# The last layer's loop over further expert tiles, moved from behind the last tile to in front of it

## The chip, the cores and the metric

The kernel runs on one core of a Trainium2 chip. The metric is device time in microseconds (us) of one execution. Three timed runs of the kernel before gave a median of 1104.19 us (1102.88 to 1104.58). The kernel is written in Python on a framework that orders the instructions of each engine with a scheduler of its own and sets all semaphores.

## The reference

The reference is a diffusion backbone of two layers over 256 latent tokens and 256 context tokens of width 1024, in float32. Each layer modulates and normalises its input, projects it, runs three groups of attention heads in parallel, projects back and adds with a layer norm. Then comes the part that this change is about, a mixture of experts with a second residual and layer norm:

```python
g_idx = argmax(h @ w_rg + b_rg)                   # one of 4 groups per token
top_v, top_i = top_k(expert logits in the group, 2)   # two of its 8 experts
combine = one_hot(expert_id, 32) * (softmax(top_v) * g_w), summed over the two
for e in range(32):
    hidden = silu(h @ w1[e]) * (h @ w3[e])        # 1024 -> 256
    out = out + combine[..., e:e+1] * (hidden @ w2[e])  # 256 -> 1024
x = layer_norm(ALPHA * x + g2 * out) * ln2_g + ln2_b
```

In the last layer only the 256 latent tokens go through it, and x is the output.

## The kernel before

**Tiles.** The mixture is computed on the tokens that chose each expert and no others. `passes(l)` lists the tiles of a layer (`todo`): each has 128 rows, shared by one, two or four experts with 128, 64 or 32 slots each. The last layer has 12 tiles, 0 to 11; tile 9 holds four experts, tiles 10 and 11 two each. Tiles go in pairs (`sets`); a pair shares a gathered input `xg` and one-hot rows `ohs`, of which there are two each, used in turn, so that pair 4 (tiles 8 and 9) has number 0 and pair 5 (tiles 10 and 11) number 1.

**One tile.** `up` (L1196) multiplies the gathered tokens with w1 and w3 of the tile's experts into a PSUM bank (L1202) and applies SiLU (L1208, L1209). `mid` (L1232) transposes the result (L1236, L1237). `back` (L1212) makes the matrix that returns rows to tokens (L1220, L1222) and the rows' weights (L1225, L1228). `down` (L1254) multiplies with w2 (L1260), weights the result (L1264) and splits it into two parts (L1265, L1266). `combine` (L1274) adds it to the residual stream X through products (L1282) and VectorE (L1289, or L1286 with sums for the layer norm, at the end). In the last layer the combine of tile i - 1 is written behind `up` of tile i, and that of tile 11 at the end. Then come the layer norm (L414 to L431) and the store (L1580).

**Weights.** An expert has three chunks of 1 MB: two of w1 and w3 (c = 0, 1), one of w2 (c = 2). They are loaded by indirect DMA on the POOL queue (L142), in the order of the tiles, into units of on-chip memory (class `Mem`, 23 units of 1 MB). `pump` issues the next ones while units are free and the cap is kept; `rel` gives a chunk's units back as soon as the tile is through with it and pumps. All loads of tiles 10 and 11 are written ahead of tile 10. At tile 10 `rows` loads two rows for the layer norm (L1463), on the POOL queue too in the last layer; some buffers of the other pair are freed just before.

**Further tiles.** If an expert has more tokens than its slots, the rest goes through a loop whose number of passes is known only on the chip: `rest` (L1494) loads it into a register on each engine (L1498) and runs a device loop (L1499). One pass finds an expert and its tokens, loads three chunks one after the other into one buffer `dyn`, and does up, mid, back, down and combine for 128 rows. The buffer is the unit of the last tile's first w2 chunk, which isn't given back at the tile's end (L1524) but behind the loop. With these inputs the loop makes no pass in the profiled execution; what is left of it are its register loads, branches and the waits at its exit, all recorded at L1498 and L1499.

**Order.** The scheduler orders instructions within the straight parts of the program; the loop divides the program into what is issued before it and what after. Within these it may issue a later instruction first where an earlier one isn't ready.

Of the kernel before, what the change touches and what calls it, by code (L numbers as in the profile page):

```python
# [117 lines left out]
def backbone(ctx: ExitStack, tc, ins, out):  # L118
# [8 lines left out]
    def bank(tag):  # L127
        return ps.tile([128, 512], F32, name="ps" + tag, tag=tag, bufs={"a": 4, "c": 2, "e": 2}[tag])

    def scratch():  # L130
        return sm.tile([128, 512], F32, name="scr", bufs=5)


    stream, slot = [], {}
# [6 lines left out]
    def dyn_load(b, idx):  # L141
        G.indirect_dma_start(out=b.ap(UNIT), out_offset=None, in_=wexp_rows,  # L142
                             in_offset=bass.IndirectOffsetOnAxis(ap=idx, axis=0),
                             bounds_check=NL * NE * 384 - 1, oob_is_err=False)

    def pump(limit=None):
        if limit is not None:
            cap[0] = limit
        while ahead[0] < len(stream):
            key, ap, n = stream[ahead[0]]  # L150
            if ap is None and key[1] not in idx_of:
                return
            if sum(x.g for x in slot.values()) + n // ROW > cap[0] * (UNIT // ROW):
                return
            b = mem.alloc(n)
            if b is None:
                return
            if ap is None:
                dyn_load(b, idx_of[key[1]][:, key[2], key[3]:key[3] + 1])
            else:  # L160
                SP.dma_start(out=b.ap(n), in_=ap)
            slot[key] = b
            ahead[0] += 1

    def take(key):
        if key not in slot:
            pump()
        return slot[key]

    def drop(key):  # L170
        slot.pop(key).free()
# [287 lines left out]
    def layer(l, first, before=None, after=None, rest_of=None):  # L459
        nb = 4 if l == 0 else 2  # L460
        nq = 128 * nb
        last = l == NL - 1
# [616 lines left out]
        for b in range(nb + lag):  # L1079
# [4 lines left out]
            if b >= lag:  # L1084
                c = b - lag
# [22 lines left out]
        xg = [mem.get(8 * 256) for _ in range(2)]  # L1108
        yo = [] if last else [mem.get(D) for _ in range(3)]
        split_y = {}  # L1110

        def parts(i):

            i = 0 if last and i < 2 else i
            if i not in split_y:
                split_y[i] = mem.get(2 * D, F32R)
            yy = split_y[i]
            return yy.v(2, 512), yy.v(2, 512, off=D)
# [3 lines left out]
        ohs = [mem.get(nb * 256, F32R) for _ in range(2)]  # L1122
# [43 lines left out]
        def onehot(q, tiles):  # L1166

            OH = ohs[q % len(ohs)].v(nb, 128 * len(tiles))
            parts = [(m, col, i * 128, 128) for i, (m, col) in enumerate(tiles)]
            if len(parts) == 2 and parts[0][0] == parts[1][0] and parts[1][1] == parts[0][1] + 128 // parts[0][0]:  # L1170
                parts = [parts[0][0:3] + (256,)]
            for b in range(nb):
                for m, col, o, n in parts:
                    e = n // m
                    V.tensor_tensor(OH[:, b, o:o + n].rearrange("p (e s) -> p e s", s=m),  # L1175
                                    iota128[:, None, 0:m].to_broadcast([128, e, m]),
                                    rk[:, b, col:col + e, None].to_broadcast([128, e, m]), OP.is_equal)

        def gather(q, n, jj):

            n *= 128
            OH, XG = ohs[q % len(ohs)].v(nb, n), xg[q % len(xg)].v(8, n)
            p = bank("c")
            pv = p[:, 0:2 * n].rearrange("p (j s) -> p j s", j=2)
            for j in range(2):
                k = jj + j
                for b in range(nb):
                    for i, H in enumerate((HHI, HLO)):
                        PE.matmul(pv[:, j, :], lhsT=H[b][:, k * 128:(k + 1) * 128], rhs=OH[:, b, :],  # L1189
                                  start=(b == 0 and i == 0), stop=(b == nb - 1 and i == 1))  # L1190
            S.activation(XG[:, jj:jj + 2, :], pv, AF.Copy)  # L1191

        def slots(m):
            return [slice(i, i + m) for i in range(0, 128, m)]

        def up(q, at, n, m, W, rel):  # L1196

            XG = xg[q % len(xg)].v(8, 128 * n)
            g = bank("a")
            for k in range(8):  # L1200
                for t, r in enumerate(slots(m)):
                    PE.matmul(g[r, :], lhsT=XG[:, k, at * 128 + r.start:at * 128 + r.stop],  # L1202
                              rhs=W(t, k // 4).v(4, 512)[:, k % 4, :], start=(k == 0), stop=(k == 7))
                if k % 4 == 3:
                    rel(k // 4)
            hab = scratch()
            ha, hb = hab[:, 0:256], hab[:, 256:512]
            S.activation(ha, g[:, 0:256], AF.Silu)  # L1208
            V.tensor_tensor(hb, ha, g[:, 256:512], OP.mult)  # L1209
            return hb  # L1210
# [244 lines left out]
        qe = len(sets) - 1  # L1455
# [17 lines left out]
        def fetch():  # L1473

            for b in range(nb):
                acc[b] = mem.get(D)
                ACC[b] = acc[b].v(D)
                two.append(mem.get(D))
                for dst, j in ((ACC[b], 0), (two[b].v(D), 1)):
                    G.indirect_dma_start(out=dst, out_offset=None, in_=ys[:, :],  # L1480
                                         in_offset=bass.IndirectOffsetOnAxis(ap=find[:, b, j:j + 1], axis=0),
                                         bounds_check=at_row, oob_is_err=False)
# [11 lines left out]
        def rest(dyn, par):  # L1494

            oht.append(mem.get(nb * 128, F32R))
            parts(2)
            r = nc.values_load(lpi[0:1, 0:1], min_val=0, max_val=32)  # L1498
            with tc.For_i(0, r, 1):  # L1499
                further(35)  # L1500

                def load(c):
                    if c < 3:
                        dyn_load(dyn, idx[:, NE, c:c + 1])

                load(0)
                onehot(par, [(128, 35)])
                for jj in range(0, 8, 2):
                    gather(par, 1, jj)
                hb = up(par, 0, 1, 128, lambda t, c: dyn, lambda c: load(c + 1))  # L1510
                ws = back(par, 0, 1, 128, 35, 2)
                down(mid(hb), ws, 128, lambda t, c: dyn, lambda c: None, 2)
                combine([2])

        end = len(todo) - 1
        for i, (m, col, e, _, go) in enumerate(todo):
            q, at_ = i // 2, i % 2
            n = len(sets[q])

            def W(t, c):  # L1520
                return take(("exp", l, e + t, c))

            def rel(c):
                if go and (i != end or c < 2):  # L1524
                    for t in range(128 // m):
                        drop(("exp", l, e + t, c))
                    pump()

            if i == end - 3:
                cap[0] = HC[0] if not last else cap[0] - 2  # L1530
            if i == end - 1:
                for k in [xg.pop((qe + 1) % 2), ohs.pop((qe + 1) % 2)] + yo:
                    k.free()
                if last:
                    rows()
                else:
                    cap[0] = HC[1]
                    rows_g2()
            if i == end:
                cap[0] = HC[2] if not last else 12  # L1540
            if at_ == 0 and q < qe:
                onehot(q + 1, [x[0:2] for x in sets[q + 1]])
            if i == away and away:
                fetch()
            hb = up(q, at_, n, m, W, rel)
            if i and not away:
                combine([(i - 1) % 2])
            if i == away and away:
                fold()
                rows()  # L1550
            if i == 1:
                lists()
            pieces = [jj for jj in range(4 * at_, 4 * at_ + 4, 2) if q < qe]
            if i < away and pieces:
                gather(q + 1, len(sets[q + 1]), pieces.pop(0))
            hc = mid(hb)
            for jj in pieces:
                gather(q + 1, len(sets[q + 1]), jj)
            if i < away:
                put(i, hc, m, W, rel)  # L1560
            else:
                ws = back(q, at_, n, m, col, i % 2)
                down(hc, ws, m, W, rel, i % 2)
        held = [("exp", l, e + t, 2) for t in range(128 // m)]
        rest(slot[held[0]], qe % 2)
        for k in held:
            drop(k)
        pump()
        fin = [end % 2] if last else [0, 1]
        combine(fin, range(2), True)  # L1570
        for k in [iw] + xg + ohs + hh + [oht.pop(2), split_y.pop(2)]:
# [121 lines left out]
```

## Time and profile before

| | |
|---|---|
| median of three runs | 1104.19 us (1102.88 to 1104.58) |
| the profiled execution, whole | 1108.46 us |
| its span in the profile | 1106.6 us, 14809 instructions |
| mean granted TensorE clock | 0.961 |
| busy: TensorE / VectorE / ScalarE / POOL | 998.9 / 512.7 / 349.3 / 305.2 us |
| moved by DMA | 300.54 MB, mean 272 GB/s |

All times in the rows are microseconds from the start of the span, unless marked ns. PE is TensorE's product, PEld its load of weights into the array, DVE VectorE, ACT ScalarE, POOL GpSimd, SP the sync engine; a q behind the name is the engine's sequencer, which waits, branches and issues DMAs. What stands behind an arrow `<-` ended an engine's idle time. The clock column PEclk is the share of full speed that TensorE was granted.

### The profile page before, as it was taken

The page shows a single profiled execution, that of the slowest core. Times are in us where ns is not written, and L with a number is a line of the kernel's source. Part 1 is how long each engine was busy: PE and PEld are TensorE (multiplying, and loading weights), DVE is VectorE, ACT ScalarE, POOL GpSimd, SP SyncE. Part 2 cuts the span into 40 slices and gives each one's busy share as a digit, 9 for nine tenths or more (in the row PEclk, how much of TensorE's full clock was granted, in tenths as well). Part 3 has the DMA queues.
Part 4 walks back from the last instruction along what each step waited for, and adds up shares of the span by engine and source line. Part 5 has one row for each costly group of instructions (what it writes and reads, how often), then busy time and mean ns, then how long its engine had stood idle before and what let it go on. Part 6 is the DMA issues. An engine that isn't in the chain of part 4 may idle for free. (4 is left out here: it accounts for less than half of the span.)

```text
span 1106.6 us, 14809 instructions
## 1 busy us (share of the span) xinstructions
PE 998.9 (90%) x5525; PEld 577.0 (52%) x5525; DVE 512.7 (46%) x1364; ACT 349.3 (32%) x708; POOL 305.2 (28%) x325
## 2 busy tenths in 40 slices
PE   4899999999999999999983789999997899999894
PEld 2689744466866454444430378844466554433231
DVE  4653457775567211100016687267655654242244
ACT  3543155572442011111111385144544222111111
POOL 2021143340000433243333132042300045334420
PEclk9999999999999999999996889999987899999997
DMA  9813147601169999999999653446325799999992
GB/s 372 321 37 115 48 181 275 230 27 51 76 267 374 398 400 423 351 412 422 423 422 414 235 183 119 172 162 216 127 78 232 302 378 421 421 422 420 422 420 94
DMA packets 46208, 300.54 MB, mean 272 GB/s; under 512 B 5395, under 2 KB 5779, under 8 KB 14389
## 3 DMA queue, kind: packets, MB, share of 16 engines
q0 software_dynamic: 25824, 177.81, 39.2%
q1 hardware_dynamic: 20308, 121.75, 29.3%
q8 instruction: 45, 0.74, 0.3%
q14 instruction: 31, 0.25, 0.1%
HBM read 292.19 MB, written 7.34 MB: 271 GB/s over the span
## 5 line engine op out<-in xcount | busy, mean ns | idle before, releaser
L142 POOL DMA_INDIRECT u<-in_w_exp,u x162 | 162.5, 1003 | 305.5 <-PE psa L1202 100.1
L1202 PE MATMUL psa<-u,u 128*32 128x512 f32 (+2 forms) x1040 | 218.1, 602 | 23.8 <-DMA u<-in_w_exp,u 23.7
L1202 PEld LDWEIGHTS psa<-u,u 128*32 128x32 f32 (+2 forms) x1040 | 65.5, 127 | 152.7 <-issue 110.6
L455 PE MATMUL psa<-u,u 128*128 128x512 f32 (+3 forms) x400 | 142.8, 360 | 0.9 <-ACT u L504 0.7
L456 PE MATMUL psa<-u,u 128*128 128x512 f32 (+3 forms) x400 | 141.7, 355 | 2.0 <-DVE u L450 2.0
L457 PE MATMUL psa<-u,u 128*128 128x512 f32 (+3 forms) x400 | 140.3, 354 | 0.1
L1189 PEld LDWEIGHTS psc<-u,u 128*128 128x128 f32 x640 | 83.6, 198 | 33.2 <-issue 30.1
L1189 PE MATMUL psc<-u,u 128*128 128x256 f32 x640 | 94.3, 298 | 3.0 <-DVE u L1175 2.1
L887 POOL TENSOR_SCALAR u<-u,ri 128x512 f32<-128x512 f32 (+1 forms) x48 | 68.5, 1431 | 99.2 <-DVE ri L885 81.7
L1209 DVE TENSOR_TENSOR scr<-scr,psa 128x256 f32<-128x256 f32 x26 | 10.9, 421 | 168.5 <-ACT scr L1208 168.5
L456 PEld LDWEIGHTS psa<-u,u 128*128 128x128 f32 x400 | 77.3, 193 | 12.9 <-DVE u L450 4.2
L455 PEld LDWEIGHTS psa<-u,u 128*128 128x128 f32 x400 | 77.1, 193 | 11.5 <-ACT u L504 1.1
L457 PEld LDWEIGHTS psa<-u,u 128*128 128x128 f32 x400 | 76.5, 192 | 9.8 <-issue 1.2
L884 ACT ACTIVATE u<-psa,nm 128x512 f32<-128x512 f32 (+1 forms) x96 | 58.4, 615 | 55.0 <-DVE nm L882 50.1
L1260 PE MATMUL pse<-u,scr 128*64 128x512 f32 (+1 forms) x288 | 67.4, 599 | 0.6 <-DMA u<-in_w_exp,u 0.6
L1208 ACT ACTIVATE scr<-psa 128x256 f32<-128x256 f32 x26 | 10.0, 385 | 175.8 <-PE psa L1202 175.8
L450 DVE TENSOR_TENSOR u<-u,u 128x1024 fp32r<-128x1024 f32 (+4 forms) x38 | 56.2, 1485 | 19.5 <-ACT u L449 19.4
L1191 ACT ACTIVATE u<-psc 128x512 f32<-128x512 f32 x52 | 31.1, 597 | 101.9 <-PE psc L1189 59.6
L882 DVE TENSOR_REDUCE nm<-psa 128x1 f32<-128x512 f32 (+1 forms) x80 | 53.2, 683 | 13.1 <-PE psa L872 9.5
L1247 PE MATMUL pse<-u,scr 128*32 128x512 f32 (+2 forms) x232 | 57.3, 600 | 1.4 <-ACT scr L1237 1.4
L419 POOL TENSOR_TENSOR lns<-lns,mhalf 128x1 f32<-128x1 f32 x22 | 15.3, 699 | 156.4 <-DVE lns L418 126.2
L449 ACT ACTIVATE u<-u 128x1024 fp32r<-128x1024 f32 (+4 forms) x38 | 47.5, 1266 | 14.2 <-PE psa L456 4.6
(317 smaller groups left out, 1361.6 us busy)
## 6 DMA issues: line engine op xcount, KB each, us to landing
u<-in_w_mod SPq DMA_DIRECT2D x48, 1024.0 KB, 6.0
u<-in_w_exp SPq DMA_DIRECT2D x30, 1024.0 KB, 7.2
u<-in_w_out SPq DMA_DIRECT2D x8, 1024.0 KB, 4.8
ys<-u SPq DMA_DIRECT2D x12, 512.0 KB, 8.1
u<-in_w_in_b SPq DMA_DIRECT2D x10, 512.0 KB, 11.8
u<-in_w_in_v SPq DMA_DIRECT2D x4, 960.0 KB, 4.6
u<-in_w_in_qa SPq DMA_DIRECT2D x4, 768.0 KB, 11.4
u<-in_ln_rows SPq DMA_DIRECT2D x6, 512.0 KB, 7.1
```

What stands on the lines that cost most here:

```text
L142: G.indirect_dma_start(out=b.ap(UNIT), out_offset=None, in_=wexp_rows, in_offset=bass.IndirectOffsetOnAxis(ap=idx, axis=0), bounds_check=N ...
L450: V.tensor_tensor(l_[:, c], w[:, c], h[:, c].bitcast(F32), OP.subtract)
L455: PE.matmul(p, lhsT=a[0], rhs=b[0], start=first, stop=False)
L456: PE.matmul(p, lhsT=a[0], rhs=b[1], start=False, stop=False)
L457: PE.matmul(p, lhsT=a[1], rhs=b[0], start=False, stop=final)
L882: V.tensor_reduce(out=nm[:, s, 0:n], in_=pv, axis=AX.X, op=OP.max, negate=True)
L884: S.activation(P[:, i, :], pv[:, i, :], AF.Exp, bias=nm[:, s, i:i + 1], accum_out=su[:, s, i:i + 1])
L887: (G if s == 0 else V).tensor_scalar(P[:, i, :], P[:, i, :], ri[:, s, i:i + 1], None, op0=OP.mult)
L1189: PE.matmul(pv[:, j, :], lhsT=H[b][:, k * 128:(k + 1) * 128], rhs=OH[:, b, :], start=(b == 0 and i == 0), stop=(b == nb - 1 and i == 1))
L1202: PE.matmul(g[r, :], lhsT=XG[:, k, at * 128 + r.start:at * 128 + r.stop], rhs=W(t, k // 4).v(4, 512)[:, k % 4, :], start=(k == 0), stop=(k ...
L1247: PE.matmul(y[r, :], lhsT=hc[:, c * 128 + r.start:c * 128 + r.stop], rhs=W(t, 2).v(2, D)[:, c, f * 512:f * 512 + 512], start=(c == 0), sto ...
L1260: PE.matmul(y[r, :], lhsT=hc[:, c * 128 + r.start:c * 128 + r.stop], rhs=W(t, 2).v(2, D)[:, c, f * 512:f * 512 + 512], start=(c == 0), sto ...
```

## The change

In the last layer the loop over further tiles is written at the start of the pass for tile 11, ahead of its `up`, and no longer behind its `down`. It uses the unit of tile 10's first w2 chunk, so tile 10 keeps its w2 chunks (`keep`) until the loop is behind it, and tile 11 gives all of its own back. The loop gathers into the buffers of pair 4 instead of those of pair 5, so these aren't freed at tile 10 in the last layer. The first layer keeps its loop behind the last tile.

```diff
--- before.py
+++ after.py
@@ -1512,7 +1512,15 @@
                 down(mid(hb), ws, 128, lambda t, c: dyn, lambda c: None, 2)
                 combine([2])
 
+        def further_tiles(held, par):
+            rest(slot[held[0]], par)
+            for k in held:
+                drop(k)
+            pump()
+
         end = len(todo) - 1
+
+        keep = end - 1 if last else end
         for i, (m, col, e, _, go) in enumerate(todo):
             q, at_ = i // 2, i % 2
             n = len(sets[q])
@@ -1521,7 +1529,7 @@
                 return take(("exp", l, e + t, c))
 
             def rel(c):
-                if go and (i != end or c < 2):
+                if go and (i != keep or c < 2):
                     for t in range(128 // m):
                         drop(("exp", l, e + t, c))
                     pump()
@@ -1529,7 +1537,7 @@
             if i == end - 3:
                 cap[0] = HC[0] if not last else cap[0] - 2
             if i == end - 1:
-                for k in [xg.pop((qe + 1) % 2), ohs.pop((qe + 1) % 2)] + yo:
+                for k in yo if last else [xg.pop((qe + 1) % 2), ohs.pop((qe + 1) % 2)] + yo:
                     k.free()
                 if last:
                     rows()
@@ -1542,6 +1550,8 @@
                 onehot(q + 1, [x[0:2] for x in sets[q + 1]])
             if i == away and away:
                 fetch()
+            if i == end and last:
+                further_tiles(held, (qe + 1) % 2)
             hb = up(q, at_, n, m, W, rel)
             if i and not away:
                 combine([(i - 1) % 2])
@@ -1556,16 +1566,15 @@
             hc = mid(hb)
             for jj in pieces:
                 gather(q + 1, len(sets[q + 1]), jj)
+            if i == keep:
+                held = [("exp", l, e + t, 2) for t in range(128 // m)]
             if i < away:
                 put(i, hc, m, W, rel)
             else:
                 ws = back(q, at_, n, m, col, i % 2)
                 down(hc, ws, m, W, rel, i % 2)
-        held = [("exp", l, e + t, 2) for t in range(128 // m)]
-        rest(slot[held[0]], qe % 2)
-        for k in held:
-            drop(k)
-        pump()
+        if not last:
+            further_tiles(held, qe % 2)
         fin = [end % 2] if last else [0, 1]
         combine(fin, range(2), True)
         for k in [iw] + xg + ohs + hh + [oht.pop(2), split_y.pop(2)]:
```

## Rows read from the trace of the kernel before

**Rows 1.** The page: busy time of each engine, and DMA share in 40 slices.

```profile
PE 998.9 (90%) x5525; PEld 577.0 (52%) x5525; DVE 512.7 (46%) x1364; ACT 349.3 (32%) x708; POOL 305.2 (28%) x325
...
DMA  9813147601169999999999653446325799999992
```

**Rows 2.** Busy time by stretch, with count, clock and DMA share, tile 11.

```profile
core 0: us, PE busy (x) PEld busy (x) DVE busy (x) ACT busy (x) POOL busy (x), PEclk, DMA share, GB/s
1072.20:1083.00 10.80, 10.39 (x40) 3.55 (x38) 4.51 (x7) 1.27 (x3) 0.00 (x0) 1.00 0.96 395
```

**Rows 3.** Timeline of PE, tiles 10 and 11: start, us, line, what.

```profile
1068.47 3.70 PE L1260 MATMUL pse<-u,scr 128*64 128x512 f32 x16
...
1073.62 2.29 PE L1282 MATMUL psa<-u,u 128*128 128x512 f32 x7 [0.21 <-DVE u L1266]
1075.84 7.08 PE L1202 MATMUL psa<-u,u 128*64 128x512 f32 x30
1083.85 0.44 PE L1236 MATMUL psa<-ident,scr 128*128 128x128 f32 x2 [0.93 <-DVE scr L1209]
...
1084.82 3.70 PE L1260 MATMUL pse<-u,scr 128*64 128x512 f32 x16
1090.62 1.19 PE L1282 MATMUL psa<-u,u 128*128 128x512 f32 x4 [2.10 <-ACTq L1499]
```

**Rows 4.** Timeline of DVE at the end.

```profile
1074.34 2.56 DVE L1289 TENSOR_TENSOR u<-u,psa 128x512 f32<-128x512 f32 x4
...
1091.62 0.69 DVE L1266 TENSOR_TENSOR u<-scr,u 128x512 fp32r<-128x512 f32 x1 [1.70 <-PE psa L1282]
1092.22 0.68 DVE L1286 SCALAR_TENSOR_TENSOR u<-psa,u 128x512 f32<-128x512 f32 x1
...
1094.47 0.69 DVE L1286 SCALAR_TENSOR_TENSOR u<-psa,u 128x512 f32<-128x512 f32 x1
```

**Rows 5.** Waits of SP at the end: us in total, times, longest.

```profile
SPq L1499 <- DMA u<-in_w_exp,u: 184.2, 2, 181.7
...
SPq L1499 <- DVEq L1498: 5.0, 1, 5.0
...
SPq L1499 <- DMA u<-in_ln_rows: 2.3, 2, 1.2
```

**Rows 6.** The loop's line, 1040 to 1095: durations in ns, first and last start.

```profile
L1499 PEldq EVENT_SEMAPHORE  x13: 51/51/51, 1088.6 to 1090.3; - x13
```

**Rows 7.** Timeline of POOL at the end.

```profile
1062.90 0.99 POOL L142 DMA_INDIRECT u<-in_w_exp,u  x1 [1.49 <-DMA u<-in_w_exp,u]
...
1067.37 0.55 POOL L1463 DMA_DIRECT2D u<-in_ln_rows  x1 [1.64 <-DMA u<-in_w_exp,u]
```

**Rows 8.** DMA issues from 1000 on: KB each, median us to landing.

```profile
u<-in_ln_rows POOLq DMA_DIRECT2D x2, 512.0 KB, 17.1
...
u<-in_w_exp,u POOLq DMA_INDIRECT x26, 19.1
```

**Rows 9.** Timeline of PE in the first layer, by that layer's loop.

```profile
605.63 6.13 PE L1202 MATMUL psa<-u,u 128*64 128x512 f32 x14 [1.80 <-DMA u<-in_w_exp,u]
```

**Rows 10.** Busy time by stretch there (columns as in rows 2).

```profile
586.00:602.00 16.00, 0.13 (x2) 0.13 (x2) 12.03 (x11) 3.44 (x3) 5.86 (x5) 0.63 1.02 415
606.00:610.60 4.60, 4.60 (x12) 1.18 (x9) 0.00 (x0) 0.00 (x0) 0.00 (x0) 0.50 0.72 297
610.60:612.00 1.40, 1.16 (x4) 0.14 (x1) 0.00 (x0) 0.20 (x1) 0.00 (x0) 0.98 0.00 0
```

**Rows 11.** The loop's line in the first layer.

```profile
L1499 POOLq EVENT_SEMAPHORE  x13: 43/43/11182, 597.6 to 619.7; - x13
```

**Rows 12.** DMA issues from 895 to 900.

```profile
u<-in_w_exp,u POOLq DMA_INDIRECT x2, 9.0
```

**Rows 13.** The page: DMA issues of the whole span.

```profile
u<-in_w_out SPq DMA_DIRECT2D x8, 1024.0 KB, 4.8
```

## The prediction

> **What bounds the kernel now.** I read the page first. TensorE is busy nine tenths of the span, and the DMA engines are full in most slices from the middle of the kernel on, down to the last but two [rows 1]. The change is in the last layer's mixture of experts alone, so I then read its last 50 us by stretches and line by line. While tile 11 (the last one) goes through its up product, TensorE is busy 10.39 of 10.80 us and the DMA engines 0.96 of the time [rows 2]: both are near full, and the DMA stream of expert weights runs out only then. Tile 11 is three steps on TensorE: up (L1202, from 1075.84 for 7.08 us), the small products from L1236 on (1083.85), down (L1260, 1084.82 for 3.70 us, to 1088.52) [rows 3]. Behind it stands the loop over further tiles, which makes no pass here: TensorE next does the combine products (L1282) at 1090.62, after 2.10 us of idleness that the profile puts to L1499, the loop's line. VectorE closes the chain: four final adds (L1286) from 1092.22, the last one at 1094.47 [rows 4], then the layer norm and the store.
>
> The view that decides is the one of waits on SP. SP has nothing to do between its arrival at the loop and the end of the kernel, so it shows what the loop's exit waits for: 184.2 us on two landings of expert weights (longest 181.7), 2.3 us on the two landings of the norm rows (L1463), and 5.0 us on VectorE's reaching the loop [rows 5]. So a loop that makes no pass still holds its engines until every DMA that was issued in front of it has landed, loads that the loop doesn't use included. TensorE runs the same 13 waits [rows 6]. In the kernel before these landings cost nothing: the norm rows are the last DMA, issued at 1067.37 with 17.1 us to landing, so at about 1084.5, while TensorE arrives at 1088.52 [rows 3, 7, 8].
>
> **The change part by part.** The loop moves from behind tile 11 to in front of its up product.
>
> *Removed at the end.* Without the loop the end of tile 11 runs like the end of tile 10. There the down products end at 1072.17 (1068.47 + 3.70) and the first L1289 add starts at 1074.34, 2.17 us later; behind the loop the same step (1088.52 to 1092.22) takes 3.70 us [rows 3, 4]. The four L1286 take 2.95 us with a gap (to 1095.17); without one, as the four L1289 show (2.56 us, plus a last accumulator read of about 0.1), 2.65. So the end gains (3.70 - 2.17) + (2.95 - 2.65) = 1.83 us. Between 1.5 (the gap stays) and 2.1 (all of TensorE's idleness).
>
> *Added in front of tile 11.* TensorE is through with tile 10 at 1072.17. POOL has by then issued every load of tile 11 and both norm rows (the last load at 1062.90, the last row at 1067.37, [rows 7]); these stand ahead of the loop in the source of both, and their buffers don't depend on tile 11. So the loop's exit waits for all of them, to 1084.5. The rows' landings are not the last of the 13 waits; the engines' own stand behind them, some seven, at 0.051 us each plus issue and a branch, which I take as 0.9 us in all (between 0.4, seven waits by their own durations, and 2.1, the whole idleness of before; the first is nearer, since the engines have long arrived) [rows 3, 6]. TensorE starts again at about 1085.4. It has idled for 13.2 us.
>
> *Its clock.* The other loop place shows the like: in layer 0 TensorE did 0.13 us of work from 586 to 602, waiting for weights, and the 14 up products from 605.63 ran in 6.13 us at a granted clock of 0.50 (the 1.2 GHz level) up to 610.6, then at 0.98 [rows 9, 10]. So about 5 us of work at half rate, which loses 2.4 us. Between 0 (the clock stays) and 3.8 (the whole up product at half rate for 7.5 us).
>
> *Tile 11 behind the loop.* Up takes 7.5 us (32 products; the timeline shows 30 in 7.08 [rows 3]), 9.9 with the clock, so it ends at 1095.3. The combine products of tile 10 (8 of L1282, 2.5 us; seven took 2.29) ran in front of tile 11's up; they write the stream that the loop's combine also writes, so they come behind the loop now. They can fill the 0.93 us that TensorE idles before L1236 and push the rest back by 1.6 us (between 0, if the adds and copies around hide them, and 2.5). From up's end to the end of down is 5.60 us (1082.92 to 1088.52), all weights being there. Down ends at 1095.3 + 1.6 + 5.6 = 1102.5 in place of 1088.5: 14.0 us later. No cover is left to lose here: VectorE and ScalarE wait for TensorE throughout.
>
> *The buffers.* The weights' buffer lent to the loop is tile 10's and not tile 11's; two units stay held a little longer, and two gather buffers and one-hot sets aren't freed before the norm rows are allocated. All weights have been issued by then, so nothing is delayed by it; I take 0 (at worst the row that lands last comes one load step of 2.48 us later, which would add that much to the loop's wait; at best it lands that much earlier). Layer 0 keeps its loop where it is: 0.
>
> *Sum.* + 14.0 - 1.8 = + 12.2 us on the profiled execution, whose span is 1106.6 us and whose whole time, 1108.46, is 4.3 us above the median 1104.19 of the runs shown. On the median: 1104.2 + 12.2 = 1116.4. With the low ends (clock 0, combine hidden) it is + 8.2, so 1112.4; with the high ends of clock, combine and exit + 15.7, so 1119.9.
>
> **The rivals.** What is written in front of the loop needn't be issued in front of it: L1266 at 1091.62 runs behind the loop and is written before it [rows 4], because the program's order is a scheduler's.
>
> *The last loads slip behind the loop.* Then the landings in front of it are over when TensorE arrives, its exit costs 2.1 us as before (1074.3), and POOL issues the last four loads (those up to 1062.90) only then. Two loads into a queue that had just run empty took 9.0 us to land [rows 12] and further ones follow at the step of 2.48 us: the second half of up can start at 1074.7 + 9.0 + 2.5 = 1086.2, takes 3.6 us (to 5.4 at the low clock), 1.9 more to down, and 3.7 for down: 1095.4 to 1097.2, so + 5.0 to + 6.8 after the gain at the end, 1109.2 to 1111.0. For it: the L1266 above. Against: POOL had those loads out 9 us before TensorE got there, and L1266 lagged because its input wasn't ready, while these buffers are free.
>
> *They slip, and land fast.* The page's direct loads of the same 1 MB took 4.8 us to land [rows 13]; at that price the same case comes out 4.2 us lower, 1105.0 to 1106.8. Against it stands the 9.0 of the very kind of load [rows 12]. The Trainium skill (DMA: Bandwidth & Descriptors, Anatomy of one DMA) puts one DMA of POOL's path at 2.0 us plus its bytes over 436 GB/s, an estimate of 4.4 us for 1 MB, by which this case would be some 0.4 us lower still.
>
> *The loop slides back.* The scheduler runs tile 11 in front of it, so that it doesn't do what it says. Only tile 10's combine then comes later, four L1289 (2.56 us) on the chain: 1106.8. Against: the up product's bank would have to pass the loop's own.
>
> *The exit doesn't hold for DMAs* (the other side). If TensorE leaves after engines alone, at 1074.3, the loads stream on under it; up then starts 0.5 to 1.4 us late (part of the combine falls into later idleness) and the end gains 1.8: - 0.4 to - 1.3, so 1102.9 to 1103.8, and 1102.1 at best if the exit's 2.1 us are all saved. It decides from the point where the waits of SP on landings turn out to be SP's alone. For it: nothing waited for these DMAs before but SP and POOL. Against: TensorE has the same 13 waits, and in layer 0 POOL stood 11.18 us in one wait of that line [rows 11].
>
> **How the numbers follow.** The forecast gets 0.70, the slipped loads 0.09, those that land fast 0.03, the loop that slides back 0.10, the exit without landings 0.08. The time is the likeliest's, 1116.4. A range of 1108.5 to 1120.0 takes in the forecast's own (1112.4 to 1119.9) and the slipped loads, and leaves the other three out, which is 0.21. A measurement of this kernel tells about 0.2% (2.2 us) from no change: slower is the forecast, the slipped loads and half of the sliding loop, 0.84; faster 0.03, out of the exit without landings; the rest, 0.13, within.
>
> **What would show it.** In the changed kernel TensorE should idle from the end of tile 10's down products for some 13 us, with L1499 or the rows' landing as its releaser; the up products behind it should run at a granted clock of 0.5 at first; L1282 should follow the last down products within about 1 us, and no L1499 should stand there. POOL should show its last weight load at about 1063 as before. The prediction is wrong if TensorE passes the loop before 1083, or if weight loads are issued after it.

## The result, and the profile after

The changed kernel takes 1113.66 us (median of four runs, 1112.04 to 1114.05), the kernel before 1104.21 beside it (four runs, 1102.88 to 1104.58). The ratio is 1.0085, with a 95% interval of 1.0068 to 1.0102: 9.45 us slower (7.5 to 11.3). The forecast was 1116.4, in a range of 1108.5 to 1120.0, with 0.84 on slower.

The profiled execution of the changed kernel took 1112.04 us whole, with a span of 1110.3. That of before lay 4.3 us above its own median, so the two can't be subtracted as they stand: in front of the change both run the same instructions in the same order, and the run of before is 7.1 us late there. It is also later than every other execution in this document (they reach that point between 1061.35 and 1065.24); no run looked for the reason. All comparisons below therefore start from one point, the first down product of tile 10 (L1260 at 1068.47 before [rows 3], at 1061.35 after), and count from there to the end of the span: 38.11 us before, 48.91 after, which is + 10.80. Line numbers are the same in both kernels up to the loop; behind it they shift (the store is L1589).

The page of the changed kernel first, with the lines that answer to [rows 1] (busy time of each engine, DMA share in 40 slices):

```profile
PE 994.4 (90%) x5525; PEld 574.8 (52%) x5525; DVE 512.4 (46%) x1364; ACT 349.0 (31%) x708; POOL 304.4 (27%) x325
...
DMA  9722157510369999999998643365327799999970
```

The busy times are those of before within half a per cent: no work was added. The last DMA slice fell from 2 to 0: the stream ends at the same place, and what follows it has become longer.

Next, the timeline of TensorE (start, us, engine, line, what, and in brackets the idle time before it with its releaser), which answers to [rows 3]:

```profile
1061.35 3.70 PE L1260 MATMUL pse<-u,scr 128*64 128x512 f32 x16
1078.41 8.95 PE L1202 MATMUL psa<-u,u 128*64 128x512 f32 x32 [13.36 <-issue]
1087.29 2.12 PE L1282 MATMUL psa<-u,u 128*128 128x512 f32 x8
1089.26 0.38 PE L1236 MATMUL psa<-ident,scr 128*128 128x128 f32 x2
...
1090.42 3.65 PE L1260 MATMUL pse<-u,scr 128*64 128x512 f32 x16
1094.01 1.10 PE L1282 MATMUL psa<-u,u 128*128 128x512 f32 x2
1095.93 1.64 PE L1282 MATMUL psa<-u,u 128*128 128x512 f32 x6 [0.82 <-ACT u L1265]
```

TensorE idles 13.36 us between tile 10's down and tile 11's up. The profile names no releaser for it ("issue"), though it named L1499 for the idle time at the loop before [rows 3]. The chain of waits says who it was; it is followed back from the first up product (start, us, what):

```profile
1059.90 0.34 DVE scr L1209
1060.23 17.11 DMA u<-in_ln_rows
1077.35 1.06 issue
1078.41 8.95 PE psa L1202 x32
```

The second norm row, issued at 1060.23, lands at 1077.35, and TensorE starts 1.06 us later. That TensorE itself stands in these landings shows at the loop's line, the view that answers to [rows 6] (durations in ns: least, median, most; then first and last start):

```profile
L1499 PEldq EVENT_SEMAPHORE  x13: 51/51/1027, 1065.1 to 1078.1; - x13
```

One of its 13 waits now takes 1.03 us, where before none took more than 0.051; by the trace it ends with the second row's landing, and seven more waits stand behind it. SP's waits agree, the view that answers to [rows 5] (engine, line, what it waited for: us in all, times, longest):

```profile
SPq L1499 <- DMA u<-in_w_exp,u: 183.3, 2, 180.9
...
SPq L1499 <- DMA u<-in_ln_rows: 2.3, 2, 1.2
```

The waits on landings are those of before; the 5.0 us on VectorE's reaching the loop has gone, since VectorE now gets there before the DMAs are through. POOL's timeline, which answers to [rows 7]:

```profile
1055.76 0.98 POOL L142 DMA_INDIRECT u<-in_w_exp,u  x1 [1.51 <-DMA u<-in_w_exp,u]
1058.01 0.57 POOL L1463 DMA_DIRECT2D u<-in_ln_rows  x1 [1.26 <-DMA u<-in_w_exp,u]
1060.23 0.55 POOL L1463 DMA_DIRECT2D u<-in_ln_rows  x1 [1.65 <-DMA u<-in_w_exp,u]
```

The last weight load is issued 5.58 us ahead of tile 10's down products, as before (1062.90 against 1068.47). Nothing slipped behind the loop.

The clock behind the pause is in the table of stretches (columns as in [rows 2]):

```profile
1065.05:1078.40 13.35, 0.00 (x0) 0.00 (x0) 2.04 (x3) 1.25 (x2) 0.00 (x0) 0.63 0.82 336
1078.40:1080.00 1.60, 1.59 (x4) 0.53 (x6) 0.00 (x0) 0.00 (x0) 0.00 (x0) 0.50 0.01 5
...
1081.00:1082.00 1.00, 1.00 (x6) 0.35 (x4) 0.00 (x0) 0.00 (x0) 0.00 (x0) 0.50 0.00 0
1082.00:1087.40 5.40, 5.40 (x27) 1.63 (x23) 0.00 (x0) 0.00 (x0) 0.00 (x0) 0.98 0.00 0
```

TensorE starts again at a granted clock of 0.50 (the 1.2 GHz level) and has it for some 3.6 us; then it is at the 2.4 GHz level. At the end VectorE's timeline, which answers to [rows 4]:

```profile
1088.17 2.47 DVE L1289 TENSOR_TENSOR u<-u,psa 128x512 f32<-128x512 f32 x4
...
1095.14 0.69 DVE L1286 SCALAR_TENSOR_TENSOR u<-psa,u 128x512 f32<-128x512 f32 x1
...
1096.93 0.69 DVE L1286 SCALAR_TENSOR_TENSOR u<-psa,u 128x512 f32<-128x512 f32 x1 [0.33 <-PE psa L1282]
...
1098.16 0.69 DVE L1286 SCALAR_TENSOR_TENSOR u<-psa,u 128x512 f32<-128x512 f32 x1
```

From the end of down (1094.07) to the end of the last L1286 (1098.85) it takes 4.78 us, where before it took 6.65 (1088.52 to 1095.17): the loop's crossing at the end has gone. The parts have changed too: the first add comes 1.07 us behind down (before 3.70), and the four adds take 3.71 us (before 2.95), with 1.10 us between the first and the second.

### The profile page after: what moved, and what is told of

Its sections match the earlier page's. It is cut to its first block, busy times and chain, and to the rows that moved or that the text cites. A ratio compares the mean times of both kernels' runs of the same rounds, so it can differ in the third digit from the quotient of the medians.

```text
span 1110.3 us, 14804 instructions
## 1 busy us (share of the span) xinstructions
PE 994.4 (90%) x5525; PEld 574.8 (52%) x5525; DVE 512.4 (46%) x1364; ACT 349.0 (31%) x708; POOL 304.4 (27%) x325
## 5 line engine op out<-in xcount | busy, mean ns | idle before, releaser
L1202 PE MATMUL psa<-u,u 128*32 128x512 f32 (+2 forms) x1040 | 217.1, 605 | 35.1 <-DMA u<-in_w_exp,u 21.7
L1202 PEld LDWEIGHTS psa<-u,u 128*32 128x32 f32 (+2 forms) x1040 | 66.0, 128 | 163.4 <-issue 125.3
L1209 DVE TENSOR_TENSOR scr<-scr,psa 128x256 f32<-128x256 f32 x26 | 10.9, 421 | 179.4 <-ACT scr L1208 179.4
L1260 PE MATMUL pse<-u,scr 128*64 128x512 f32 (+1 forms) x288 | 67.3, 599 | 0.6 <-DMA u<-in_w_exp,u 0.6
```

The source lines that it names most:

```text
L1260: PE.matmul(y[r, :], lhsT=hc[:, c * 128 + r.start:c * 128 + r.stop], rhs=W(t, 2).v(2, D)[:, c, f * 512:f * 512 + 512], start=(c == 0), sto ...
```

## The experiments

Two theories were put against each other. **Landings:** the exit of a loop that makes no pass holds every engine until all DMAs issued in front of it have landed, so the price is set by the last landing. **Fixed price:** leaving the loop there costs a stall of its own (registers, branches, a restart), whatever the queue holds. The first five columns count from the first L1260 of tile 10, in us of one profiled execution each, and the ratio is against the kernel before on the same chip. For the change that is the pair above. The median of before, of 23 runs each, is 1101.74 us beside four of the kernels (the rows behind the loop, one more load, before without its loop, the loop in front of down) and 1103.0 beside the other four. The ratio isn't the quotient of the two medians; it differs from that by up to 0.001.

| kernel | up starts | up takes | down starts | last add ends | span ends | timed: median, ratio (95%) |
|---|---|---|---|---|---|---|
| before | 3.48 | in two parts | 16.34 | 26.69 | 38.11 | 1104.21 |
| the change | 17.07 | 8.95 | 29.08 | 37.50 | 48.91 | 1113.66, 1.0085 (1.0068 to 1.0102) |
| rows behind the loop | 15.08 | 8.55 | 26.68 | 35.10 | 46.54 | 1109.81, 1.0071 (1.0051 to 1.0091) |
| one more load in front | 19.64 | 8.86 | 31.56 | 39.98 | 51.48 | 1115.35, 1.0114 (1.0094 to 1.0133) |
| before, no loop | 3.48 | in two parts | 16.34 | 24.87 | 36.59 | 1101.68, 0.999 (0.9978 to 1.0002) |
| the change, no loop | 3.48 | in two parts | 16.34 | 24.86 | 36.57 | 1101.77, 0.9985 (0.9971 to 0.9999) |
| loop in front of down | 3.49 | in two parts | 18.39 | 26.82 | 38.24 | 1103.51, 1.0006 (0.999 to 1.0021) |
| products in front of the loop | 17.03 | 7.09 | 27.18 | 35.60 | 47.01 | 1111.96, 1.0085 (1.0069 to 1.0101) |
| weights behind the loop | 5.83 | in four parts | 26.14 | 34.66 | 46.08 | 1111.29, 1.0073 (1.0052 to 1.0094) |
| loop in front of mid | 3.49 | in two parts | 17.39 | 27.58 | 39.02 | 1103.06, 0.9995 (0.9981 to 1.0009) |

**The norm rows behind the loop.** This takes the last two landings away from the loop: the loads that land last in the changed kernel are issued behind it, and land while up runs.

```diff
                 if last:
-                    rows()
+                    pass
...
                 further_tiles(held, (qe + 1) % 2)
+                rows()
             hb = up(q, at_, n, m, W, rel)
```

> The changed kernel, with the two norm rows' loads written behind the loop. Theory (landings): the loop's exit holds TensorE until the last DMA issued in front of it has landed; that is now tile 11's last weight load, 2.5 us before the rows (1074.9 and 1077.4 in the profile of the changed kernel). TensorE idles 10.9 us in place of 13.4, time 2.5 us under the changed kernel's 1113.7: 1111.2. Rival (fixed price): crossing the loop in mid-stream costs what it costs whatever is in flight; idle 13.4 us, 1113.7.

The chain of waits of this kernel, at the loop:

```profile
1055.87 19.14 DMA u<-in_w_exp,u
1075.01 1.52 issue
1076.52 1.97 PE psa L1202 x3
```

The releaser is now the last weight load. Counted from tile 10's down it lands 2.44 us earlier than the second row did (13.56 against 16.00), which is about one load step of 2.48. Idle time falls less, from 13.36 to 11.37 us, where 10.9 was expected: from the landing to the first product it now takes 1.52 us in place of 1.06, and by the trace ten of TensorE's 13 waits stand behind this landing where seven stood behind the row's. The stretch falls by 2.37 (48.91 to 46.54), of which 1.99 is the earlier start and 0.40 the shorter up. The timed runs can't tell it: their ratio of 1.0071 overlaps that of the change.

**One more load in front of the loop.** The other way round: a load of 1 MB that nobody uses, issued behind the norm rows.

```diff
                     rows()
+                    extra = mem.get(UNIT)
+                    G.dma_start(out=extra.ap(UNIT), in_=wexp[l, 0, 0])
...
                 further_tiles(held, (qe + 1) % 2)
+                extra.free()
```

> The changed kernel, with one more load of 1 MB, which nothing uses, issued behind the norm rows and in front of the loop. Theory (landings): the last landing comes one step, 2.5 us, later; TensorE idles 15.8 us, time 1116.2. Rival (fixed price): nothing needs the load, 13.4 us and 1113.7.

```profile
1065.05 16.87 DMA u<-in_w_exp
1081.92 1.17 issue
1083.09 1.11 PE psa L1202
```

```profile
L1499 PEldq EVENT_SEMAPHORE  x13: 51/51/3606, 1067.2 to 1082.7; - x13
```

The chain of waits names the useless load, and TensorE's longest wait at the loop, 3.61 us, ends with its landing. Idle time rises to 15.94 us, the stretch by 2.57; the timed ratio overlaps that of the change here too. Taken away or added, loads that tile 11 doesn't need move tile 11's start, by 1.99 and 2.57 us. A fixed price would have left 13.4 us in both.

**Without the last layer's loop, from either kernel.** The loop over further tiles of the last layer is left out, once from the kernel before, once from the changed one, and with it the freeing of two buffers that only the loop allocates.

```diff
-        rest(slot[held[0]], qe % 2)
+        if not last:
+            rest(slot[held[0]], qe % 2)
...
```

```diff
         def further_tiles(held, par):
-            rest(slot[held[0]], par)
+            if not last:
+                rest(slot[held[0]], par)
...
```

> The kernel before, with the last layer's loop left out (further tiles aren't computed; with these inputs there are none). It prices the loop behind the last tile. From the end of tile 10 in the trace: 1.8 us, so 1102.4 against 1104.2, and no idle of 2.1 us between the last down products and the combine. If the loop's price there was hidden by the end of tile 11 anyway: 1104.2.

> The changed kernel with the loop left out of the last layer, and the rest of the change kept: tile 10's w2 chunks held one tile longer, two gather buffers and one-hot sets freed later, norm rows in other memory. If the loop's place is all that the change costs, from tile 10's down to the end 36.6 us, as in the kernel before without its loop, and the same time, about 0.1% under the kernel before. If the buffers cost something it is longer by that.

Both come to the same stretch, 36.59 and 36.57 us, in one execution each. So the loop is worth 1.52 us where it stood and 12.34 where it stands now, and everything else in the change (which unit is lent, which buffers are freed later) makes 0.02 us there. Of the 1.8 us that were expected, 1.82 are there at the last add (24.87 against 26.69); 0.30 is lost again behind it, where the chain of the kernel before without its loop has three waits of VectorE at L429 that the chain of the kernel before hasn't. The timeline of TensorE of the changed kernel without its loop shows tile 11 as it runs in the kernel before:

```profile
1065.24 3.70 PE L1260 MATMUL pse<-u,scr 128*64 128x512 f32 x16
1068.72 1.02 PE L1202 MATMUL psa<-u,u 128*64 128x512 f32 x2
```

**The loop in front of tile 11's down.** By then the rows have landed, so the landings theory leaves the crossing alone to be paid.

```diff
-            if i == end and last:
-                further_tiles(held, (qe + 1) % 2)
             hb = up(q, at_, n, m, W, rel)
...
                 ws = back(q, at_, n, m, col, i % 2)
+                if i == end and last:
+                    further_tiles(held, (qe + 1) % 2)
                 down(hc, ws, m, W, rel, i % 2)
```

> The loop later in tile 11: behind its up, mid and back, in front of its down, with tile 10's buffer as in the change. Theory (landings): the last landing (1084.5 by the trace of the kernel before) is over when TensorE gets there (1084.8), so the exit costs some 1.0 to 1.5 us and the end gains 1.8: 0.3 to 0.8 us under the kernel before, 1103.4 to 1103.9. Rival (fixed price of a crossing in the middle, 9 to 11 us net): 1113.

TensorE's timeline:

```profile
1083.06 3.65 PE L1260 MATMUL pse<-u,scr 128*64 128x512 f32 x16 [2.03 <-issue]
```

The last row landed at 1080.71, and TensorE came to the loop at 1081.03. It idles 2.03 us, about what it idled at the end before (2.10 [rows 3]) and more than the 1.0 to 1.5 expected, and 1.92 of it comes back from there on (19.85 from down's start to the end of the span, before 21.77): 38.24 against 38.11, so the expected gain isn't there. The time is the same as before (1.0006, 0.999 to 1.0021). Crossing the loop in the middle of a tile doesn't cost 9 to 11 us by itself.

**Products in front of the loop.** To weigh the clock by itself, TensorE multiplies data that are at hand into a bank that nobody reads (24 calls, 48 records in the trace, two of which ran ahead of tile 10's down) while it would wait.

```diff
             if i == end and last:
+                XG, g = xg[q % len(xg)].v(8, 128 * n), bank("c")
+                for k in range(12):
+                    for t, r in enumerate(slots(m)):
+                        PE.matmul(g[r, :], lhsT=XG[:, k % 8, r.start:r.stop],
+                                  rhs=slot[held[t]].v(4, 512)[:, k % 4, :], start=True, stop=True)
                 further_tiles(held, (qe + 1) % 2)
```

> The changed kernel, with 24 products of the up product's shape, which nothing reads, in front of the loop, where TensorE idles 13.4 us. Theory (landings and clock): the exit waits for the last landing all the same, so the 11.3 us of added products cost nothing; TensorE idles 2.1 us, and tile 11's up product behind the loop runs at the full clock, 7.5 us in place of 8.95: 1.4 us under the changed kernel. If the loop's price were a fixed one on TensorE's own arrival: 11.3 us over the changed kernel. If the clock doesn't matter: the same as the changed kernel.

Its timeline of TensorE, and one stretch of its table:

```profile
1066.01 10.52 PE L1557 MATMUL psc<-u,u 128*64 128x512 f32 x46
1079.56 7.09 PE L1202 MATMUL psa<-u,u 128*64 128x512 f32 x32 [3.03 <-issue]
```

```profile
1079.50:1086.60 7.10, 7.04 (x33) 2.23 (x33) 0.00 (x0) 0.00 (x0) 0.00 (x0) 1.00 0.00 1
```

The added products ended at 1076.53, before the second row landed (1078.50), so TensorE idles 3.03 us and not the 2.1 expected; it starts 1.06 us behind the landing, as in the change. Up starts at the same place (17.03 against 17.07) and takes 7.09 us at a clock of 1.00, in place of 8.95: the clock's part is 1.86 us, and the stretch falls by 1.90. The runs can't tell so little (1.0085 both).

**Weights behind the loop.** The loads of tile 11 are held back until the loop is written; five of its six then are issued behind it. That builds the rival of the prediction in which the last loads slip, with five loads in place of its four.

```diff
-        while ahead[0] < len(stream):
+        while ahead[0] < len(stream) and ahead[0] != stop[0]:
...
+        if last:
+            stop[0] = len(stream) - 6
...
             if i == end and last:
+                stop[0] = None
                 further_tiles(held, (qe + 1) % 2)
```

> The changed kernel, with tile 11's weight loads written behind the loop (one of the six may still be issued ahead of it). Theory (landings): TensorE crosses the loop some 2 us after tile 10, and then idles in its up product for loads that start from an empty queue. If such a load lands 9.0 us after its issue and the next ones 2.48 us apart, the end comes 1 to 2 us before that of the changed kernel; if 4.8 us, 5 to 6 us before it. Slower than the kernel before in both. Rival (fixed price): the loop costs as in the changed kernel and the late loads come on top, slower than it by 5 us or more.

The norm rows' loads, too, are issued earlier in this kernel, 15 us earlier counted from tile 10's down. Three lines more stand in front of the loop, so L1202 is L1205 here. Its timeline of TensorE, two stretches of its table, then the DMA issues of the first microsecond behind the loop and of all five (the last column is the median from issue to landing):

```profile
1069.74 1.57 PE L1205 MATMUL psa<-u,u 128*64 128x512 f32 x2 [2.12 <-ACTq L1502]
...
1076.03 5.81 PE L1205 MATMUL psa<-u,u 128*64 128x512 f32 x14 [3.57 <-DMA u<-in_w_exp,u]
...
1082.43 1.07 PE L1205 MATMUL psa<-u,u 128*64 128x512 f32 x2
...
1084.57 3.65 PE L1205 MATMUL psa<-u,u 128*64 128x512 f32 x14
```

```profile
1072.50:1076.00 3.50, 0.00 (x0) 0.00 (x0) 0.69 (x1) 0.00 (x0) 2.59 (x4) 0.50 0.91 344
1076.00:1082.00 6.00, 5.97 (x15) 1.78 (x16) 0.00 (x0) 0.00 (x0) 0.56 (x1) 0.63 0.97 389
```

```profile
u<-in_w_exp,u POOLq DMA_INDIRECT x1, 5.6
```

```profile
u<-in_w_exp,u POOLq DMA_INDIRECT x5, 9.3
```

The landings in front of the loop are over (the last at 1067.46, and TensorE comes to it at 1067.62), and the exit costs 2.12 us as at the end before: the same loop at the place of the change, with an empty queue. So the place alone doesn't cost 13.4 us; the loads in flight at it do. But now the stream has stopped, and tile 11 waits for what it asked for late, another 3.57 us at once and then a low clock (0.50 from 1070.2 to 1080.4): + 7.97 us on the stretch, 1.0073 timed. That is 2.83 us under the change, between the two cases that were expected (1 to 2 and 5 to 6 us under it). Held back or awaited, these loads cost most of the change's price.

**The loop in front of mid, the rows behind it.** Behind up TensorE idles 0.93 us in any case [rows 3], so a crossing of 2 us there should cost 1.1 and give 1.5 to 1.9 back at the end.

```diff
                 if last:
-                    rows()
+                    pass
...
-            if i == end and last:
-                further_tiles(held, (qe + 1) % 2)
             hb = up(q, at_, n, m, W, rel)
             if i and not away:
                 combine([(i - 1) % 2])
+            if i == end and last:
+                further_tiles(held, (qe + 1) % 2)
+                rows()
```

> The loop between up and mid of tile 11, where TensorE idles 0.93 us in any case, and the norm rows' loads behind it, so that the last landing in front is tile 11's last weight load, 0.9 us before the up product ends. Theory (landings): no wait on DMA, the exit costs about 1.0 us over the idle that is there, the end gains 1.85: 0.8 us under the kernel before (0.07%, less than the timing tells; in the trace from tile 10's down to the end 37.3 in place of 38.1 us). Rival (fixed price): as the changed kernel, 9 us slower.

Its timeline of TensorE, and the stretch of its down products:

```profile
1078.37 0.44 PE L1236 MATMUL psa<-ident,scr 128*128 128x128 f32 x2 [2.03 <-DVEq L1499]
...
1079.29 5.37 PE L1260 MATMUL pse<-u,scr 128*64 128x512 f32 x16
```

```profile
1079.30:1082.00 2.70, 2.70 (x9) 0.91 (x10) 0.49 (x3) 0.00 (x0) 0.13 (x1) 0.61 0.87 235
1082.00:1084.70 2.70, 2.66 (x10) 0.75 (x6) 0.75 (x1) 0.09 (x1) 0.00 (x0) 0.75 0.38 156
```

The crossing behaves: 2.03 us in place of 0.93. But the down products then run at 0.61 and 0.75 of the clock and take 5.37 us for 3.70, which eats the gain: the stretch is 39.02, 0.9 above before, and the time is the same (0.9995, 0.9981 to 1.0009). With the clock up it would be 37.35 by estimate (39.02 less 5.37 - 3.70), 0.8 us better than before and less than these runs can tell; no run shows it. No version with the loop in it beat the kernel before by more than its measurement tells.

## Why the prediction was right, step by step

- **The exit waits for landings.** Forecast: TensorE held until the last norm row has landed, then about 0.9 us, 13.2 us idle in all. Measured: 13.36 idle, 1.06 from landing to product, with seven waits between as assumed. Shown by the extra load (start + 2.57), by the rows behind the loop (start - 1.99) and by crossings of 2.03, 2.03 and 2.12 us where the landings were over. The prediction took TensorE's waits for the landings from their number [rows 6]; TensorE's own longest waits, 1.03 and 3.61 us, now end with them. The rival in which the exit doesn't hold for DMAs is out.
- **Up, 9.9 us forecast, 8.95 measured.** This is the term that was mis-sized most. Its undisturbed length is 7.09 us (with the clock kept up) and not 7.5: I had added the two products in front to the thirty of [rows 3] at full length. The clock costs 1.86 and not 2.4; the low clock was taken as long as in the first layer [rows 10], some 5 us, and was 3.6. The high end of 3.8 for the clock is half rate for 7.5 us and not, as it says, the whole up product at half rate, which would lose some 7; the range didn't cover that, and it didn't happen.
- **Tile 10's combine behind up, + 1.6 forecast, + 1.16 measured.** From the end of up to down it is 3.06 us in place of 1.90: the combine's products take 2.12 us rather than 2.5, and 0.93 of that falls into the idle time ahead of L1236, as forecast.
- **The end, - 1.83 forecast, - 1.87 measured, out of other parts.** TensorE is not held behind the last down products, and L1282 follows them at once. But the forecast had 1.53 from the way to the first add and 0.30 from the adds; measured, the way is 2.63 shorter and the adds take 0.76 longer. VectorE began to weight tile 11's result (L1264) 1.66 us ahead of down's end, at 1092.41, where before it was 0.86 ahead: the first half of the adds comes early, and the second waits. That the sum agrees is partly luck. In the kernel before without its loop the parts are as forecast: 2.15 us to the first add, 2.67 for the four.
- **The buffers, 0 forecast.** Both kernels without the loop agree within 0.02 us, in one trace each.
- **The sum.** + 12.2 forecast, + 10.80 measured on the stretch: 0.95 of the difference of 1.4 is up, 0.44 the combine, and the exit's + 0.14 (up starts at 17.07 against 16.93) and the end's 0.04 nearly cancel with the down products, 0.05 shorter. The timed 9.45 has an interval of 7.5 to 11.3, which holds 10.80 and not 12.2.
- **The rivals.** POOL's last load left at its old place, so neither form of the slipping loads took place, and all 32 products of tile 11's up run behind the loop, so the loop didn't slide back. Where loads were made to slip the cost was 7.97, above the 5.0 to 6.8 forecast for it, though with five loads behind the loop and not the rival's four. The price of 9.0 us from issue to landing [rows 12] had been read wrongly: I called that queue empty, but loads issued ahead of those two were still in flight (the one issued at 888.89 landed at 900.90, theirs left at 897.36 and 898.79). The load issued at 883.37 in the kernel before had only one in front of it, which landed at 884.97; the DMA issues of that microsecond say 5.5 us, like the first one behind the loop above (5.6), whose queue was empty. Both had further loads issued behind them before they landed, so neither is the time of a load by itself:

```profile
u<-in_w_exp,u POOLq DMA_INDIRECT x1, 5.5
```

The Trainium skill (DMA: Bandwidth & Descriptors, Anatomy of one DMA) gave an estimate of 4.4 us for that load; the measured 5.5 and 5.6 decide, and they lie nearer to it than to the 9.0 that I had set against it. What made the slipped case dearer all the same: the first half of up, too, waited for a load (to 1075.99), and from there TensorE worked without a pause, at the low clock until 1080.4 (14 products in 5.81 us, where the next 14 took 3.65) and with six products of tile 10's combine among them.

## What to carry to other kernels

A device loop of this framework was a barrier for every load in flight on POOL's queue, even when it made no pass: price its place by the last landing of the loads issued ahead of it, prefetches for later work included, and not by what its body uses. Loads on other queues weren't in flight at the loop in these runs, so whether it waits for those too isn't shown. Read that price from an engine that has nothing else to do (here SP's waits at the loop's line), and look for a place where the queues have just run dry. If the landing time of a load is to be read from a trace, look first at what was in flight when it was issued.

## What the runs showed of the hardware that was not expected

The length of TensorE's idle time doesn't decide by itself whether the clock falls. After 2.03 us of idleness in front of tile 11's down it stayed at 1.00 (down 3.65 us), and after 3.03 us behind the dummy products too (up 7.09). With 2.03 us in front of mid it was at 0.61 in the down products a microsecond later (5.37 us), and with 2.12 us in the kernel with the weights behind the loop it was at 0.50 from 1070.2 to 1080.4, with a second pause of 3.57 us in that time. What tells these cases apart stays open: no run was made for it.

The norm rows' two direct loads of 512 KB, issued 0.57 us apart into the queue that the loop had emptied, landed in 4.43 and 5.09 us (the rows behind the loop), against 17.1 us behind the weights' stream [rows 8]: nearly all of the 17.1 was the queue. That is about the 4.8 us that 1 MB took on SP's queue [rows 13], but the two were in flight together, so it doesn't show what half the bytes save.
